# Order and grouping around the output products of a four-layer trunk on one core

## The chip, the core and the metric

The program runs on one core of one Trainium2 chip, in one launch. The metric is the device time of one execution in microseconds (us), from a host-side launch to completion. A profiled execution also leaves a trace: the span in it runs from the first to the last instruction of the program on the core.

Five engines work side by side, each with its own instruction stream, executed in order: PE (TensorE, matrix products and transposes), DVE (VectorE, elementwise work), ACT (ScalarE, functions of one operand and copies), POOL (GpSimd) and SP (SyncE, which here only issues DMA transfers).

## The reference, cut to what matters

A trunk of four layers on 256 tokens of width 1024, all in float32. Each layer has a token mixer and a gated feed-forward network (FFN), both fed with a normalised and modulated copy of the residual stream x:

```python
for i in range(DEPTH):                                   # 4 layers
    mod = c_act @ ada_w[i] + ada_b[i]                    # adaLN: 6 vectors of 1024
    sh1, sc1, g1, sh2, sc2, g2 = jnp.split(mod, 6, axis=-1)
    h = modulate(rmsnorm(x, mix_norm_g[i]), sh1, sc1)    # h*(1+scale)+shift
    y = mixer(h)                # layer 0, 3: gMLP; layer 1: latent attention; layer 2: HGRN2
    x = x + (1.0 + g1)[:, None, :] * y
    h = modulate(rmsnorm(x, ffn_norm_g[i]), sh2, sc2)
    x = x + (1.0 + g2)[:, None, :] * conv_ffn(h, ...)    # up 1024 -> 5632, conv, gate, down 2816 -> 1024
return rmsnorm(x, final_g)
```

Every mixer and every FFN ends in an output product into the residual stream: `go` for gMLP (2048 to 1024), `wo` for the other two mixers (1024 to 1024), `dn` for the FFN (2816 to 1024).

## The kernel before

**Split precision.** Each float32 factor is split into a high and a low part (`fp32r`), and a product is three matmuls (`mm3`): high by high, high by low, low by high. Activations are split by `split` (ACT makes the high part, DVE the low one). Weights come as units of 128 x 2048 float32 (1 MB, tile `raw`, five buffers) by SP's DMA queue, in the order of a list, `plan`. `conv_half` converts one half of a unit: ACT casts `wh` (L209), DVE subtracts for `wl` (L210); `wh` and `wl` have five buffers of 1024 columns each. `unit()` hands out the next unit and asks, ahead of use, for later loads and conversions.

**Order.** The code is written in one order, and a planner then decides the order on each engine with its own model of costs: of the instructions that it holds to be ready it takes the one written first, so an instruction written later can be placed ahead of earlier ones that it holds to be waiting. `tc.issue_after(ins)` forces every instruction of the block on the engine of `ins` to stand behind `ins` on that engine; it says nothing about other engines. `state["chain"]` holds such instructions for conversions.

**adaLN.** The modulation vectors are worked out beside the layers. Some (`ada_vector`) are computed on DVE, one instruction for 128 rows and 1024 columns (tile `adaw`, L339, two for each load of 1 MB), the others (`ada_tensor`) on PE as 16 narrow matmuls for each load (tile `adaps`, L317). `pacing`, called by `unit()`, loads and runs them at rates from a table; `need` runs all that a stage must have. `GAPS` gives, stage by stage, how many loads of the PE kind are kept back; `modulated` runs them at the join between two stages.

**A layer.** `modulated(l, which)` transposes the normalised x on PE (`xt`, L464), modulates (`nt`, L473, on DVE) and splits it into `hh` and `hlo`, in eight chunks of 128 features; while it does so, it asks for one half of a conversion. The mixer or the FFN follows. In `ffn` 22 chunks of `up` (48 matmuls of 256 columns each) go into four PSUM banks (`acc`), and ACT and DVE make the causal convolution, the gate and the split of each chunk (`y`, `g`, `gh`, `gl`, L1169 to L1175). The first step of a chunk that reads its bank starts when all of the chunk's matmuls are done.

**Output products.** The output is token-major: two token tiles of 128 and two halves of 512 columns, so four accumulators (`acc`, the same four banks). A unit of weights holds two K chunks of 128. `out_product` runs over the K chunks and, inside, over the four accumulators; only the last unit (in the last layer's `dn` the last two) goes accumulator by accumulator, and each finished one is passed to `residual`: multiply by the gate row (`gated`, L500), add to x (L501), squares (L502). After both halves of a token tile `root` works out the inverse root, and `scaled` writes the normalised tile to `gx`, half on DVE (L455), half on ACT (L456). `gx` holds, in its second half, the gate row: `gate_load` asks for it before the output product (in the `wo` products at their second unit), from ten buffers with the tag `big`.

Of the kernel before, what the change touches and what calls it, by code (L numbers as in the profile page):

```python
# [18 lines left out]
D = 1024  # L19
# [8 lines left out]
GAPS = [3, 0, 4, 3, 5, 3, 3, 0]  # L28
# [16 lines left out]
HGO = "o0 o1 s0 a0 o2 s1 a1 n0 o3 s2 n1 w0 s3 n2 w1 n3 w2 w3"  # L45
ADA_P = [(0, 5), (1, 2), (1, 3), (2, 4), (2, 5), (3, 2), (3, 5)]
# [44 lines left out]
def build(ctx, tc, A, out, stages=None):  # L91
# [99 lines left out]
    def conv_half():  # L191

        if not halves:
            if state["dma"] == state["conv"]:
                if state["dma"] == len(plan):
                    return
                dma_next()
            raw, n = raws.pop(0)
            ready.append([])
            halves.extend((raw, o, min(1024, n - o), state["conv"]) for o in range(0, n, 1024))  # L200
            state["conv"] += 1
        raw, o, w, n = halves.pop(0)
        wh = wp.tile([P, 1024], F32R, tag="wh", name=f"wh{n}_{o}", bufs=5)
        wl = wp.tile([P, 1024], F32R, tag="wl", name=f"wl{n}_{o}", bufs=5)
        with contextlib.ExitStack() as es:

            for ins in state["chain"]:
                es.enter_context(tc.issue_after(ins))
            act.copy(wh[:, :w], raw[:, o : o + w])  # L209
            i = dve.tensor_tensor(wl[:, :w], raw[:, o : o + w], wh[:, :w].bitcast(F32), op=ALU.subtract)  # L210
            state["sub"] = getattr(i, "ins", i)
        ready[-1].append((wh, wl))
# [114 lines left out]
    def ada_vector(l, u):  # L327
# [3 lines left out]
        def load(i):  # L331
# [3 lines left out]
            def run():  # L335
                for e in range(2):
                    b = 8 * u + 2 * i + e
                    c0 = col("ada_b", l * 48 + b)
                    dve.tensor_tensor_reduce(raw[:, e, :], raw[:, e, :], cbc[:], 1.0, prm[:, c0 : c0 + 1], ALU.mult, ALU.add,  # L339
                                             mod[:, l, b : b + 1])  # L340
                if i == 3:
                    mod_post(l, 8 * u, 8)
# [109 lines left out]
    def scaled(t, rs):  # L452

        xn = cur["gx"][:, t, :]
        dve.tensor_scalar_mul(xn[:, 0:512], x[:, t, 0:512], rs)  # L455
# [14 lines left out]
    def modulate_chunk(l, which, c, xt):  # L470
        b = 24 * which + c
        t = t1("nt")
        dve.tensor_scalar(t[:], xt, amul[:, l, which, c : c + 1], mod[:, l, b : b + 1], op0=ALU.mult, op1=ALU.add)  # L473
        split(hh[:, c, :], hlo[:, c, :], t[:])

    def modulated(l, which):
# [15 lines left out]
    def residual(t, f, ps, last):  # L492
# [7 lines left out]
        dve.tensor_tensor(g[:], ps, gx[:, 1, s], op=ALU.mult)  # L500
        dve.tensor_tensor(x[:, t, s], x[:, t, s], g[:], op=ALU.add)  # L501
# [30 lines left out]
    def out_product(name, k0, units, yh, yl, last, fin_=False):  # L532

        kcs = range(k0, k0 + 2 * len(units))
        if k0 == 0:
            cur["ps"] = [acc(f"{name}{i}") for i in range(4)]
        ps = cur["ps"]

        def one_(kc, t, f):
            a, b = hl(units[(kc - k0) // 2], kc % 2 * D + 512 * f, 512)  # L540
            ts = slice(t * P, t * P + P)
            mm3(ps[2 * t + f][:], yh(kc)[:, ts], yl(kc)[:, ts], a, b, kc == 0, kc == last)

        tf = [(t, f) for t in range(2) for f in range(2)]
        if last not in kcs:
            for kc in kcs:
                for t, f in tf:
                    one_(kc, t, f)
                if kc == k0:
                    flush(mid=1)  # L550
        else:

            for t, f in tf:
                for kc in kcs:
                    one_(kc, t, f)
                residual(t, f, ps[2 * t + f][:], fin_)

    def split(h, lo, src):
        act.copy(h, src)  # L559
        dve.tensor_tensor(lo, src, h.bitcast(F32), op=ALU.subtract)  # L560
# [84 lines left out]
    def gmlp(l, j, start=None):  # L645
# [91 lines left out]
        gate_load(l, 0)  # L737
        for i in range(8):
            w = unit(LAST if i == 7 else None)
            out_product("go", 2 * i, [w], yh, yl, 15)  # L740
# [189 lines left out]
    class OutProj:  # L930
# [5 lines left out]
        def step(self, i):  # L936
            if i == 1:
                gate_load(self.l, 0)
            w = unit(LAST if i == 3 else None)
            out_product("wo", 2 * i, [w], self.yh, self.yl, KC - 1)  # L940
# [219 lines left out]
    def ffn(l):  # L1160
        gh, gl = hilo("g", NF)
        for c in range(NF):
            ps = proj_pair(hk, lk, KC, f"up{c}", c < KOUT)
# [12 lines left out]
            split(gh(c), gl(c), g[:])  # L1176
# [9 lines left out]
        gate_load(l, 1)  # L1186
        i = 0
        while i < NF // 2:
            w = [unit(LAST if i == NF // 2 - 1 else None)]
            if last and i == NF // 2 - 2:  # L1190
                w.append(unit())
            out_product("dn", 2 * i, w, gh, gl, NF - 1, last)
            i += len(w)
# [35 lines left out]
    for kind, l in stages:  # L1229
# [3 lines left out]
        if kind == "mix":  # L1233
# [3 lines left out]
            if l % 3 == 0:  # L1237
                if quick:
# [4 lines left out]
                    def start(chunk):  # L1243
                        for step in FIRST.split():
# [10 lines left out]
                            if step[0] == "a":  # L1255
# [5 lines left out]
                                modulate_chunk(l, 0, c, xt[0][:, c % 2, :])  # L1261
# [112 lines left out]
```

## Time and profile before

| what | value |
|---|---|
| median of 3 runs | 1383.8 us (1382.55 to 1386.59) |
| the profiled execution's own time | 1384.63 us |
| its span, first to last instruction | 1382.8 us |
| mean granted TensorE clock | 0.985 |
| ACT busy | 776.2 us (56%) |
| POOL busy | 18.0 us (1%) |
| moved by DMA | 330.69 MB, mean 239 GB/s |

A line of the profile names the kernel line (L339), the engine, the operation and the tiles it writes and reads (`adaw<-adaw,cbc,prm`). A row of the timeline begins with the start and the duration in us from the start of the span; a number in brackets at its end is the idle time of the engine just before, and what ended it. The granted clock is the share of TensorE's full clock that the chip gave in that stretch; 0.50 is half speed. The end of a matmul is modelled, since matmuls overlap: start-to-start times tell how fast PE goes.

### The profile page before, as it was taken

How to read it: one execution, taken by the hardware profiler on the slowest of the kernel's cores; microseconds unless marked ns; L12 is line 12 of the kernel's file. 1: busy time of each engine (PE TensorE's matmuls, PEld its weight loads, DVE VectorE, ACT ScalarE, POOL GpSimd, SP SyncE). 2: the span in 40 equal slices, each digit the busy share in tenths (PEclk: the TensorE clock that was granted, in tenths of full speed). 3: DMA queues.
4: the chain of work that ended last, by engine and by line, in shares of the span. 5: the costliest groups of instructions: out<-in, count | busy, mean ns of one | idle time of the engine just before them, and what ended most of it. 6: DMA issues, size and time to landing. Idle time of an engine off the chain costs nothing.

```text
span 1382.8 us, 24847 instructions
## 1 busy us (share of the span) xinstructions
PE 1329.4 (96%) x10092; PEld 1195.7 (86%) x10092; DVE 1123.6 (81%) x1818; ACT 776.2 (56%) x1220; POOL 18.0 (1%) x27
## 2 busy tenths in 40 slices
PE   7999989999999999979999999999899999999997
PEld 6799779998787899968797879998777998899986
DVE  4699698888887889797878989889976874888854
ACT  3763366664456666534585646665445744666643
POOL 0100000000000000000000000000001000000000
PEclk8999999999999999999999999999999999999999
DMA  9868955566957366598565586567876465455640
GB/s 383 328 243 312 412 178 183 214 214 266 424 215 292 146 227 237 182 350 337 183 241 186 197 337 214 184 214 289 333 307 228 158 251 185 153 183 184 214 152 31
DMA packets 49162, 330.69 MB, mean 239 GB/s; under 512 B 6548, under 2 KB 7572, under 8 KB 10134
## 3 DMA queue, kind: packets, MB, share of 16 engines
q1 hardware_dynamic: 47888, 327.40, 63.0%
q10 hardware_dynamic: 1160, 1.71, 0.4%
q8 instruction: 79, 1.29, 0.4%
q14 instruction: 35, 0.29, 0.1%
HBM read 328.01 MB, written 1.08 MB: 238 GB/s over the span
## 4 chain that ended last, share of the span: by engine, by line
PE 56%; DVE 9%; ACT 2%; issue 1%; ACTq 0%; DVEq 0%
PE up L240 8%; PE up L241 8%; PE up L242 8%; PE dn L240 4%; PE dn L242 4%; PE dn L241 4%; DVE adaw L339 2%; DVE wl L210 1%; PE wo L240 1%; ACT wh L209 1%; PE wo L242 1%; PE wo L241 1%; PE v L240 1%; PE v L242 1%; PE v L241 1%
## 5 line engine op out<-in xcount | busy, mean ns | idle before, releaser
L209 ACT CAST wh<-raw 128x1024 fp32r<-128x1024 f32 x418 | 433.7, 1049 | 393.5 <-PE up L241 176.0
L210 DVE TENSOR_TENSOR wl<-raw,wh 128x1024 fp32r<-128x1024 f32 x418 | 508.9, 1227 | 147.7 <-ACT wh L209 146.8
L240 PE MATMUL up<-hh,wh 128*128 128x256 f32 x1408 | 398.4, 284 | 3.4 <-DVE y L1171 2.4
L241 PE MATMUL up<-hlo,wh 128*128 128x256 f32 x1408 | 398.0, 283 | 0.4 <-DVE hlo L560 0.2
L242 PE MATMUL up<-hh,wl 128*128 128x256 f32 x1408 | 398.0, 283 | 0.1
L240 PEld LDWEIGHTS up<-hh,wh 128*128 128x128 f32 x1408 | 269.9, 192 | 5.6 <-issue 3.9
L241 PEld LDWEIGHTS up<-hlo,wh 128*128 128x128 f32 x1408 | 270.1, 192 | 1.0 <-DVE hlo L560 0.9
L242 PEld LDWEIGHTS up<-hh,wl 128*128 128x128 f32 x1408 | 270.3, 192 | 0.5 <-DVE wl L210 0.3
L339 DVE CUSTOM_DVE_ANT_0 adaw<-adaw,cbc,prm 128x1024 f32<-128x1024 f32 x120 | 151.7, 1277 | 2.7 <-DMA adaw<-adad 2.7
L240 PE MATMUL dn<-wh,gh 128*128 128x512 f32 x352 | 139.5, 398 | 13.3 <-DVE y L1171 11.8
L241 PE MATMUL dn<-wl,gh 128*128 128x512 f32 x352 | 139.1, 395 | 0.6 <-DVE wl L210 0.6
L242 PE MATMUL dn<-wh,gl 128*128 128x512 f32 x352 | 139.2, 395 | 0.0
L1169 ACT ACTIVATE y<-up,cwb 128x256 f32<-128x256 f32 x176 | 98.6, 560 | 20.8 <-DVE y L1171 20.5
L240 PEld LDWEIGHTS dn<-wh,gh 128*128 128x128 f32 x352 | 67.5, 192 | 29.9 <-issue 12.5
L1171 DVE SCALAR_TENSOR_TENSOR y<-up,cwb,y 128x254 f32<-128x254 f32 x176 | 84.7, 481 | 5.0
L1170 DVE SCALAR_TENSOR_TENSOR y<-up,cwb,y 128x255 f32<-128x255 f32 x176 | 84.0, 477 | 2.5 <-ACT y L1169 2.5
L241 PEld LDWEIGHTS dn<-wl,gh 128*128 128x128 f32 x352 | 67.4, 191 | 14.9 <-DVE wl L210 1.1
L242 PEld LDWEIGHTS dn<-wh,gl 128*128 128x128 f32 x352 | 67.2, 191 | 14.3
L240 PE MATMUL u<-hh,wh 128*128 128x256 f32 x256 | 74.0, 289 | 0.0
L241 PE MATMUL u<-hlo,wh 128*128 128x256 f32 x256 | 72.4, 283 | 0.0
L242 PE MATMUL u<-hh,wl 128*128 128x256 f32 x256 | 72.4, 283 | 0.0
L240 PE MATMUL v<-wh,hh 128*128 128x512 f32 x128 | 51.9, 408 | 3.0 <-ACT hh L559 2.5
(331 smaller groups left out, 2052.3 us busy)
## 6 DMA issues: line engine op xcount, KB each, us to landing
raw<-up SPq DMA_DIRECT2D x88, 1024.0 KB
adaw<-adad SPq DMA_DIRECT2D x60, 1024.0 KB
raw<-dn SPq DMA_DIRECT2D x44, 1024.0 KB
adaw<-adap SPq DMA_DIRECT2D x28, 1024.0 KB
raw<-gmu SPq DMA_DIRECT2D x16, 1024.0 KB
raw<-gmo SPq DMA_DIRECT2D x16, 1024.0 KB
raw<-gmv SPq DMA_DIRECT2D x15, 1024.0 KB
adaf<-ada SPq DMA_DIRECT2D x8, 1024.0 KB
```

The lines of the kernel that those rows point to most:

```text
L209: act.copy(wh[:, :w], raw[:, o : o + w])
L210: i = dve.tensor_tensor(wl[:, :w], raw[:, o : o + w], wh[:, :w].bitcast(F32), op=ALU.subtract)
L240: pe.matmul(ps, lh, rh, start=start, stop=False)
L241: pe.matmul(ps, lh, rl, start=False, stop=False)
L242: i = pe.matmul(ps, ll, rh, start=False, stop=stop)
L339: dve.tensor_tensor_reduce(raw[:, e, :], raw[:, e, :], cbc[:], 1.0, prm[:, c0 : c0 + 1], ALU.mult, ALU.add, mod[:, l, b : b + 1])
L1169: act.activation(y[:], ps[:, e, :], AF.Identity, bias=b, scale=w[2])
L1170: dve.scalar_tensor_tensor(y[:, 1:], ps[:, e, : S - 1], w[1], y[:, 1:], op0=ALU.mult, op1=ALU.add)
L1171: dve.scalar_tensor_tensor(y[:, 2:], ps[:, e, : S - 2], w[0], y[:, 2:], op0=ALU.mult, op1=ALU.add)
```

## The change

- **First unit tile by tile.** In all output products the first unit runs accumulator by accumulator over its two K chunks; before, only the last did.
- **Chunks held at the end.** In `go` and `dn` the last three K chunks (four in the last layer's `dn`, as before) run accumulator by accumulator with `residual` behind each; before, two. The `wo` products still hold two.
- **Gate asked for later.** `gate_load` comes four units before the end of `go` and `dn` instead of before their first unit, and at the third unit of `wo` instead of the second. For the FFN `gx` now lies in a `raw` buffer.
- **`scaled`.** Token tile 0 is scaled by DVE alone, in one instruction of 1024 columns.
- **Order constraints.** In `residual` the first multiplication stands behind the last conversion and the last adaLN update written so far on DVE, each later one behind the addition before it. Conversions written after the first two chunks of `modulated` stand behind those chunks' modulation (DVE) and high part (ACT). In `ffn` the conversions and DVE's adaLN updates written in chunk c stand behind the last DVE step (`gl`) of chunk c-2. At the start of the program the conversions' DVE step stands behind the modulation of chunk 0.
- **`GAPS`** of layer 0's `dn` goes from 0 to 2.

```diff
-GAPS = [3, 0, 4, 3, 5, 3, 3, 0]
+GAPS = [3, 2, 4, 3, 5, 3, 3, 0]
+HOLD = (3, 4)
 ...
 # conv_half, after act.copy(wh)
+            if "sub1" in state:
+                es.enter_context(tc.issue_after(state["sub1"]))
 ...
 # gate_load
-        gx = cur["gx"] = big("gx", (P, 2, D))
+        if which:
+            gx = wp.tile([P, 2, D], F32, tag="raw", name="gx", bufs=NRAW)
+        else:
+            gx = big("gx", (P, 2, D))
+        cur["gx"] = gx
 ...
 # ada_vector
+                    with contextlib.ExitStack() as es:
+                        for ins in state["chain"]:
+                            es.enter_context(tc.issue_after(ins))
+                        r = dve.tensor_tensor_reduce(raw[:, e, :], ...)
+                    state["ada"] = getattr(r, "ins", r)
 ...
 # scaled
+        if t == 0:
+            dve.tensor_scalar_mul(xn, x[:, t, :], rs)
+            return
 ...
 # modulated
-                modulate_chunk(l, which, c, xts[i][:, c - c0, :])
+                ins = modulate_chunk(l, which, c, xts[i][:, c - c0, :])
+                if c < 2:
+                    state["chain"] += ins
 ...
 # residual
-        dve.tensor_tensor(g[:], ps, gx[:, 1, s], op=ALU.mult)
-        dve.tensor_tensor(x[:, t, s], x[:, t, s], g[:], op=ALU.add)
+        with contextlib.ExitStack() as es:
+            for k in ("sub", "ada") if t == f == 0 else ("add",):
+                if k in state:
+                    es.enter_context(tc.issue_after(state[k]))
+            dve.tensor_tensor(g[:], ps, gx[:, 1, s], op=ALU.mult)
+        i = dve.tensor_tensor(x[:, t, s], x[:, t, s], g[:], op=ALU.add)
+        state["add"] = getattr(i, "ins", i)
 ...
-    def out_product(name, k0, units, yh, yl, last, fin_=False):
+    def out_unit(n, w, ps, yh, yl, i):
+        kcs = range(2 * i, 2 * i + 2)
+        order = [(kc, t, f) for t, f in TF for kc in kcs] if i == 0 else [(kc, t, f) for kc in kcs for t, f in TF]
+        for j, (kc, t, f) in enumerate(order):
+            chunk_product(n, w[kc % 2], ps, yh, yl, kc, t, f)
+            if j == 3:
+                flush(mid=1)
+    def out_end(n, held, ps, yh, yl, last=False):
+        for t, f in TF:
+            for j, w in enumerate(held):
+                chunk_product(n, w, ps, yh, yl, n - len(held) + j, t, f)
+            residual(t, f, ps[2 * t + f][:], last)
+    def tokens(units, name, yh, yl, l, which, last=False):
+        ps = [acc(f"{name}{i}") for i in range(4)]
+        held = []
+        for i in range(units):
+            if i == units - 4:
+                gate_load(l, which)
+            w = unit(LAST if i == units - 1 else None)
+            if i < units - 2:
+                out_unit(2 * units, w, ps, yh, yl, i)
+            else:
+                held += w
+                while len(held) > HOLD[last] - 2 * (units - 1 - i):
+                    for t, f in TF:
+                        chunk_product(2 * units, held[0], ps, yh, yl, 2 * units - 2 * (units - 1 - i) - len(held), t, f)
+                    held.pop(0)
+        out_end(2 * units, held, ps, yh, yl, last)
 ...
 # gmlp: the loop over out_product becomes
+        tokens(8, "go", yh, yl, l, 0)
 # OutProj.step
-            if i == 1:
+            if i == 2:
                 gate_load(self.l, 0)
 ...
 # ffn
+        done = []
         for c in range(NF):
+            if c > 1:
+                state["chain"] = (done[c - 2],)
 ...
-            split(gh(c), gl(c), g[:])
+            done.append(split(gh(c), gl(c), g[:])[1])
 ...
-        gate_load(l, 1)
-        i = 0
-        while i < NF // 2:
-            ...
+        tokens(NF // 2, "dn", gh, gl, l, 1, last)
```

More of the change, by code (lines that the diff above doesn't have):

```diff
@@ L530, in finish, with chunk_product @@
             (nc.scalar if f else nc.sync).dma_start(out[:, t, s], y[:, t, s])
-    def out_product(name, k0, units, yh, yl, last, fin_=False):
[L534 to L556, printed above, removed]
+    def chunk_product(n, w, ps, yh, yl, kc, t, f):
+        s = slice(512 * f, 512 * f + 512)
+        ts = slice(t * P, t * P + P)
+        mm3(ps[2 * t + f][:], yh(kc)[:, ts], yl(kc)[:, ts], w[0][:, s], w[1][:, s], kc == 0, kc == n - 1)
@@ new lines, in build @@
+    TF = [(t, f) for t in range(2) for f in range(2)]
+    def out_unit(n, w, ps, yh, yl, i):
[10 more added lines that the diff above has]
+            residual(t, f, ps[2 * t + f][:], last)
@@ L736, in gmlp @@
         pace("go", l)
[L737 to L740, printed above, removed]
+        tokens(8, "go", yh, yl, l, 0)
     tables = []
@@ L936, in step @@
         def step(self, i):
-            if i == 1:
+            if i == 0:
+                self.ps = [acc(f"wo{j}") for j in range(4)]
+            if i == 2:
                 gate_load(self.l, 0)
             w = unit(LAST if i == 3 else None)
-            out_product("wo", 2 * i, [w], self.yh, self.yl, KC - 1)
+            if i < 3:
+                out_unit(KC, w, self.ps, self.yh, self.yl, i)
+            else:
+                out_end(KC, w, self.ps, self.yh, self.yl)
     def hg_units():
```

21 lines of the change are left out of this document (9 added, 12 removed).

## The prediction

> **What bounds the kernel now.** I read the page first, for which engine fills the span.
>
> ```profile
> span 1382.8 us, 24847 instructions
> PE 1329.4 (96%) x10092; PEld 1195.7 (86%) x10092; DVE 1123.6 (81%) x1818; ACT 776.2 (56%) x1220; POOL 18.0 (1%) x27
> ...
> L210 DVE TENSOR_TENSOR wl<-raw,wh 128x1024 fp32r<-128x1024 f32 x418 | 508.9, 1227 | 147.7 <-ACT wh L209 146.8
> L339 DVE CUSTOM_DVE_ANT_0 adaw<-adaw,cbc,prm 128x1024 f32<-128x1024 f32 x120 | 151.7, 1277 | 2.7 <-DMA adaw<-adad 2.7
> ```
>
> TensorE (PE) is busy for 96%, DVE for 81%, and the diff removes none of its work. What can be won is time in which PE waits, and time in which it runs slowly. So the second view is the list of waits (columns: microseconds in total, times, longest).
>
> ```profile
> PE dn L240 <- DVE y L1171: 11.8, 5, 4.5
> PE xt L464 <- DVE gx L455: 8.6, 6, 5.4
> ...
> PE up L240 <- DVE y L1171: 2.4, 6, 0.4
> ...
> ACT wh L209 <- DMA raw<-gmo: 24.3, 8, 5.3
> ```
>
> The largest wait stands where a feed-forward layer changes from `up` to `dn`, the second at the joins, where an output product ends and the next stage needs its normalised input. The third view is the table by stretches, asked where I found the granted clock (after the busy times of PE, weight load, DVE, ACT and POOL) at one half; the last row is an undisturbed stretch.
>
> ```profile
> 178.40:185.10 6.70, 4.51 (x19) 3.63 (x19) 5.67 (x15) 6.29 (x14) 0.00 (x0) 0.50 0.16 65
> 608.50:615.10 6.60, 4.28 (x10) 3.44 (x11) 6.60 (x14) 0.74 (x2) 0.00 (x0) 0.50 0.96 395
> 680.20:683.40 3.20, 3.16 (x13) 2.92 (x14) 3.18 (x9) 1.60 (x4) 0.39 (x2) 0.50 0.44 184
> 970.30:973.50 3.20, 3.20 (x9) 2.53 (x8) 3.20 (x8) 0.41 (x1) 0.00 (x0) 0.50 1.00 420
> 977.20:980.40 3.20, 3.20 (x9) 2.55 (x8) 2.49 (x7) 1.27 (x3) 0.00 (x0) 0.50 0.93 361
> ...
> 630.00:668.00 38.00, 38.00 (x169) 31.48 (x168) 27.36 (x32) 14.24 (x14) 0.00 (x0) 1.00 0.83 314
> ```
>
> Each half-speed stretch stands at a wait, so a wait is paid twice: once idle, once slow.
>
> **Part 1, `up` to `dn`: the leash in `ffn`, the late gate, the first unit tile by tile.** The timeline of DVE and PE at layer 1, and two PE rows of layer 2:
>
> ```profile
> 608.60 0.48 DVE L1170 SCALAR_TENSOR_TENSOR y<-up,cwb,y 128x255 f32<-128x255 f32 x1
> 608.99 1.28 DVE L339 CUSTOM_DVE_ANT_0 adaw<-adaw,cbc,prm 128x1024 f32<-128x1024 f32 x1
> ...
> 602.63 0.47 PE L240 MATMUL dn<-wh,gh 128*128 128x512 f32 x1 [1.43 <-ACT y L1169]
> 610.82 0.77 PE L240 MATMUL dn<-wh,gh 128*128 128x512 f32 x1 [4.53 <-DVE y L1171]
> 618.00 0.47 PE L240 MATMUL dn<-wh,gh 128*128 128x512 f32 x1 [1.45 <-DVE y L1171]
> ...
> 969.00 0.47 PE L240 MATMUL dn<-wh,gh 128*128 128x512 f32 x1 [2.95 <-DVE y L1171]
> 976.78 0.54 PE L240 MATMUL dn<-wh,gh 128*128 128x512 f32 x1 [2.52 <-DVE y L1171]
> ```
>
> The four `dn` accumulators are the PSUM banks of the last four `up` chunks, and a bank is free only when DVE has read it for y. Between two steps of one y stands an adaLN update (adaw, L339), which nothing needs yet. DVE is three chunks behind when PE begins `dn`. Layer 1 loses 1.43 + 4.53 + 1.45 = 7.4 us idle and, at half clock, half of the 4.28 us worked, 2.1: 9.5. Layer 2 loses 2.95 + 2.52 = 5.5 and half of 3.20 + 3.20, 3.2: 8.7. Together 18.2.
>
> After the change, conversions and updates asked for in chunk c stand behind the last DVE step of chunk c-2, so DVE can be at most two chunks late. The leash lasts through `dn` at chunk 19, so updates can still fall between the y steps of chunks 20 and 21. The first `dn` unit needs its last bank after three tiles instead of after three matmul triples: at six matmuls of 0.225 us each (rows further down) 4.05 us instead of 2.0. The y of chunk 21 takes two ACT and four DVE steps, about 2.6 us by the 0.48 of the row; with three updates of 1.28 in its gaps 6.4. That is 2.35 us late, in two layers 4.7. Gain 18.2 - 4.7 = **13.5**; ends 0 (as many updates as before) and 18.2. The updates moved are not removed: they go to the rest of `dn`, where the undisturbed row has 38 - 27.36 = 10.6 us of free DVE for about eight of them. If that cover fails they stand before the join (part 4).
>
> Near the end of layer 1's `up`, PE waits 0.41 us in every chunk for the y of three chunks before. The leash removes that lag: gain **2.4** (ends 0 and 2.4).
>
> **Part 2, joins: three chunks held, order of residual, conversions behind the first chunks.** The join after `dn` of layer 1:
>
> ```profile
> 672.55 0.39 PE L242 MATMUL dn<-wh,gl 128*128 128x512 f32 x1
> ...
> 674.92 1.29 DVE L339 CUSTOM_DVE_ANT_0 adaw<-adaw,cbc,prm 128x1024 f32<-128x1024 f32 x1
> 675.06 0.71 ACT L456 ACTIVATE gx<-x,ss 128x512 f32<-128x512 f32 x1
> 676.20 1.27 DVE L339 CUSTOM_DVE_ANT_0 adaw<-adaw,cbc,prm 128x1024 f32<-128x1024 f32 x1
> 676.95 2.92 ACT L209 CAST wh<-raw 128x1024 fp32r<-128x1024 f32 x3
> ...
> 679.78 0.81 ACT L559 CAST hh<-nt 128x256 fp32r<-128x256 f32 x2
> 680.24 0.58 PE L240 MATMUL hf<-hh,wh 128*128 128x256 f32 x1 [1.32 <-ACT hh L559]
> ```
>
> From PE's end at 672.94 to the first product of the next stage 7.3 us pass. In the chain stand two updates, the ACT half of token tile 0 (0.71, ahead of tile 1's root) and three casts of later weights ahead of hh. The change puts the last traced update and conversion ahead of the first residual, the whole of token tile 0 on DVE (about 0.9 us by the row's two halves, beside PE's longer tiles: nine matmuls, 2.03 us, against 1.4 of DVE), and later conversions behind hh of chunk 1. The cleanest join is after `go` in layer 3:
>
> ```profile
> 1181.32 0.39 PE L242 MATMUL go<-wh,yl 128*128 128x512 f32 x1
> 1181.64 1.93 PE L317 MATMUL adaps<-adaw,cact 128*32 128x256 f32 x32
> ...
> 1186.97 0.51 PE L240 MATMUL up<-hh,wh 128*128 128x256 f32 x2
> ```
>
> It takes 5.26 us with tile 0's half still on ACT; without that about 0.4 less: 4.9 is the chain itself, and what I take for the joins that are long now. The other two long ones:
>
> ```profile
> 172.94 2.35 DVE L210 TENSOR_TENSOR wl<-raw,wh 128x1024 fp32r<-128x1024 f32 x2
> 174.18 0.39 PE L240 MATMUL go<-wh,yh 128*128 128x512 f32 x1
> 174.63 0.39 PE L242 MATMUL go<-wh,yl 128*128 128x512 f32 x1
> 180.37 1.46 PE L464 MATMUL xt<-ident,gx 128*128 128x128 f32 x5 [5.36 <-DVE gx L455]
> 184.47 0.80 PE L240 MATMUL up<-hh,wh 128*128 128x256 f32 x2
> ...
> 375.39 0.55 PE L464 MATMUL xt<-ident,gx 128*128 128x128 f32 x3 [2.11 <-DVE gx L455]
> 380.78 0.38 PE L240 MATMUL cq<-hh,wh 128*128 128x256 f32 x1
> ```
>
> (Two matmuls lie between 174.18 and 174.63, hence 0.225 us each.) After `go` in layer 0, 175.01 to 184.47 is 9.46 us; in it two conversions sit between the first product and its addition, which the new order forbids. To 4.9 it is 4.6 less; idle of that size still costs clock, 1.1 of it: **3.5**. After `dn` of layer 0, 373.28 to 380.78, 7.5 to 4.9: **2.6**. After `dn` of layer 1, 2.4 and the half-clock stretch at 680.20 (1.6): **4.0**. The two `wo` joins hold two chunks as before and the one after `dn` of layer 2 has its gap filled; I take 0.5 each for the ACT half that leaves: **1.5**. After `go` in layer 3, 0.4 is won, but the 32 filler matmuls shown there are used up earlier (GAPS for layer 0's `dn` goes from 0 to 2, where they fill the 2.11 us wait), and an unfilled gap falls to half clock for 3.2 us: 0.4 - 1.6 = **-1.2**. Sum of the joins **10.4**; ends 3 (only ACT's half is won, in seven places) and 16 (no clock loss, updates all in time).
>
> On what a gap does to the clock: the 2.11 us wait above is followed by half speed, as the stretches show for longer ones. [...]
>
> **Part 3, the start.** The first weight conversion is put behind nt of chunk 0.
>
> ```profile
> 14.27 0.80 PE L240 MATMUL v<-wh,hh 128*128 128x512 f32 x1 [2.24 <-ACT hh L559]
> ```
>
> The wait of 2.24 holds one conversion of 1.23 on DVE; about 1 us earlier, at half clock still: **0.5** (ends -0.5, since wl then comes later for the second matmul, and 1).
>
> **Part 4, what it costs.** In `dn`, gx takes one of the five raw buffers from four units before the end until the transposes are done; on SP's queue a weight load that finds no buffer holds back every load behind it, updates' weights and gate rows included. The nearest row for late weights is that of gmo, at most 5.3 us for one cast, where PE does not stop. I take 0.5 in each of four layers, **2.0** (ends 0 and 5.3 each). The first residual now waits on DVE for the last update and the last conversion; behind it queue the other residuals and the root. If two updates (2.55) come late in the joins after `dn` of layers 0 to 2, the longer tiles take back most of it; I take 0.8 each, **2.4** (ends 0 and 7.6). The gate asked for later has over 20 us until its use in `dn` and `go` (four units of 24 matmuls, 21.6 us); in `wo` only about two units, covered as long as SP isn't held: 0.
>
> Sum: 13.5 + 2.4 + 10.4 + 0.5 - 2.0 - 2.4 = **22.4** less. The profiled execution took 1384.6 us (span 1382.8 and 1.8 around it), 0.8 above the median of the three runs. Forecast 1384.6 - 22.4 = 1362.2, some 1361.5 on the scale of the median.
>
> **The rivals.**
> *The updates stay in the way.* The planner fills every gap between two dependent DVE steps; nothing ties updates to chunks 20 and 21. If two thirds of the losses of part 1 remain (gain 6 instead of 13.5) and the residuals wait their full price (7.6 instead of 2.4), the time is 1361.5 + 7.5 + 5.2 = 1374. For it: the alternation in the rows; against it: the lag of three chunks, which gave the updates their place, is cut.
> *The leash turns round (slower).* Conversions now wait for DVE's own backlog. If in `up` PE comes to wait for wl instead of y, each of 4 x 20 leashed chunks pays; from 22.4 / 80 = 0.28 us a chunk on, the change loses. At the 0.41 that the wait of the other sort cost, 33 us: 1361.5 + 33 = 1394. Against it: the chunks are 6 us, and the step waited for ends some 4 us into the chunk before the one that traces the conversion.
> *Weights come late.* With four buffers in place of five, a cast 5.3 us late at the end of each `dn` eats 19 of the 22: 1381, no change that could be told.
> *Everything fits.* All upper ends: 18.2 + 2.4 + 16 + 1 = 37.6: 1346.
>
> **How the numbers follow.** Forecast 0.64, updates stay 0.16, everything fits 0.08, weights late 0.06, leash 0.06. The range 1345 to 1377 holds the first three (0.88) less some tails. Under 0.3%, 4 us, nothing can be told from no change here. Faster 0.64 + 0.16 + 0.08 = 0.88, same 0.06, slower 0.06.
>
> **What would show it.** Right: no wait of PE dn for y above 1 us; DVE at the end of `up` with y steps back to back, and updates behind gl of chunk 19; no PE wait for y inside `up`; 4.9 us from the last output matmul to the first of the next stage; L455 with a 1024-wide form, half as many L456; fewer stretches at 0.50. Wrong: PE up waiting for wl; L500 waiting for adaw or wl in the first tile; casts waiting for DMA near the ends of `dn`.

## The result and the profile after

The changed kernel takes 1353.02 us (median of 4 runs, 1352.72 to 1353.39); the kernel before, on the same chip, 1383.84 (1382.55 to 1386.59). The ratio is 0.9775, 95% interval 0.9758 to 0.9792: some 31 us, or 2.2%, less. I had forecast 1361.5 and a range of 1345 to 1377. The time lies in the range and the sign is right; the gain is 30.8 where the sum gave 22.4.

The page of the changed kernel, and the top of its list of waits on PE (microseconds in total, times, longest), with two short rows from further down the list:

```profile
span 1351.2 us, 24627 instructions
PE 1316.6 (97%) x10092; PEld 1192.5 (88%) x10092; DVE 1112.7 (82%) x1818; ACT 773.5 (57%) x1212; POOL 17.3 (1%) x27
```

```profile
PE xt L478 <- DVE gx L467: 8.0, 4, 3.9
PE xt L478 <- DVE gx L469: 3.1, 3, 2.4
...
PE up L245 <- DVE wl L213: 0.9, 2, 0.5
...
PE dn L243 <- DVE y L1217: 0.5, 2, 0.3
```

The lines have moved: matmuls L240 to L242 are now L243 to L245, wl L210 is L213, the updates L339 are L349, y is L1216 and L1217, gx L467, L469 and L470. The 11.8 us that `dn` waited for y are 0.5, and the row of `up` waiting for y (2.4) is gone. The waits at the joins are as long as before: 8.0 and 3.1 against 8.6 and 1.1. So nearly all of the change lies between `up` and `dn`. I measured each product from the start of its first matmul to the end of its last in both traces, and each join between them (us):

| piece | before | after |
|---|---|---|
| `up`, layer 1 / 2 | 131.2 / 127.3 | 128.0 / 127.0 |
| idle between `up` and `dn`, layer 1 | 1.4 | none |
| `dn`, layer 1 / 2 | 70.3 / 70.2 | 60.5 / 60.6 |
| `go` / `dn`, layer 0 | 49.3 / 60.2 | 47.9 / 62.1 |
| joins after `go` and `dn` of layer 0 | 9.5, 7.5 | 7.5, 7.3 |
| joins after `wo` and `dn` of layer 1 | 6.2, 7.3 | 4.7, 4.7 |
| joins after `wo` and `dn` of layer 2 | 6.2, 6.2 | 7.1, 4.7 |
| join after `go` of layer 3 | 5.3 | 5.6 |
| first product starts at | 14.3 | 13.4 |

Layers 1 and 2 from `up` to `dn` give 24.5 us, the joins 6.5, the start 0.9. The other pieces take 0.4 more in all, and the span is 31.5 shorter.

**`up` to `dn`.** The timeline of DVE at layer 1, and PE's one wait there:

```profile
593.73 1.28 DVE L349 CUSTOM_DVE_ANT_0 adaw<-adaw,cbc,prm 128x1024 f32<-128x1024 f32 x1
...
596.53 0.48 DVE L1217 SCALAR_TENSOR_TENSOR y<-up,cwb,y 128x254 f32<-128x254 f32 x1
...
599.52 0.42 DVE L600 TENSOR_TENSOR gl<-g,gh 128x256 fp32r<-128x256 f32 x1
599.86 0.48 DVE L1216 SCALAR_TENSOR_TENSOR y<-up,cwb,y 128x255 f32<-128x255 f32 x1
...
601.77 1.28 DVE L349 CUSTOM_DVE_ANT_0 adaw<-adaw,cbc,prm 128x1024 f32<-128x1024 f32 x1
...
604.57 0.48 DVE L1217 SCALAR_TENSOR_TENSOR y<-up,cwb,y 128x254 f32<-128x254 f32 x1
...
605.20 0.47 PE L243 MATMUL dn<-wh,gh 128*128 128x512 f32 x1 [0.18 <-DVE y L1217]
```

The updates do still stand between the steps of the last two chunks, as the first rival said, with conversions beside them. The last y ends at 605.05, 10.4 us after the end of `up` at 594.6. But PE stands only 0.18 us: it ran 45 matmuls of `dn` first, which I read as 15 on each of three banks that were free by then. In the kernel before it ran 15, waited 4.53 us, ran 15 more and waited 1.45 us.

**The clock**, as stretches (PE, weight load, DVE, ACT, POOL, granted clock, DMA share, GB/s):

```profile
177.50:180.90 3.40, 3.32 (x16) 3.32 (x17) 2.73 (x8) 2.25 (x6) 0.00 (x0) 0.51 0.00 0
375.50:378.80 3.30, 2.97 (x16) 2.79 (x14) 2.63 (x7) 2.15 (x4) 0.00 (x0) 0.50 1.02 429
1153.80:1157.00 3.20, 3.20 (x15) 3.20 (x16) 2.61 (x7) 2.10 (x5) 0.00 (x0) 0.50 0.02 5
594.60:605.10 10.50, 10.42 (x47) 8.29 (x45) 10.50 (x20) 2.90 (x6) 0.00 (x0) 1.00 0.91 328
```

The half-speed stretches of layers 1 and 2 are gone. Besides those at the program's start and end three stay, at the three joins that still have a gap of over 2 us (3.85, 3.70 and 2.36).

**Two joins side by side.** After `go` of layer 0, then after `dn` of layer 1:

```profile
170.11 0.69 DVE L522 TENSOR_TENSOR gated<-go,gx 128x512 f32<-128x512 f32 x1 [3.92 <-PE go L245]
...
174.32 0.68 DVE L522 TENSOR_TENSOR gated<-go,gx 128x512 f32<-128x512 f32 x1
...
176.64 0.55 PE L478 MATMUL xt<-ident,gx 128*128 128x128 f32 x3 [3.85 <-DVE gx L467]
177.58 3.04 PE L478 MATMUL xt<-ident,gx 128*128 128x128 f32 x13 [0.39 <-DVE gx L469]
180.27 0.56 PE L243 MATMUL up<-hh,wh 128*128 128x256 f32 x1
...
649.23 0.68 DVE L522 TENSOR_TENSOR gated<-dn,gx 128x512 f32<-128x512 f32 x1
...
655.05 2.80 PE L324 MATMUL adaps<-adaw,cact 128*32 128x256 f32 x48
655.16 0.69 DVE L522 TENSOR_TENSOR gated<-dn,gx 128x512 f32<-128x512 f32 x1 [0.62 <-PE dn L245]
...
657.78 2.07 PE L478 MATMUL xt<-ident,gx 128*128 128x128 f32 x16
659.84 0.38 PE L243 MATMUL hf<-hh,wh 128*128 128x256 f32 x1
```

In layer 1 only the fourth `gated` is left when PE is done (655.16), fillers cover the gap, and 4.71 us pass. In layer 0 PE ends at 176.64 - 3.85 = 172.79 and the fourth `gated` starts 1.5 us later. The first one, which waits for PE, starts only 2.7 us before PE's end, against 5.9 us in layer 1. I read this as the planner running the four accumulators' last matmuls mixed, so that they end close together (the trace doesn't tell the accumulators apart; experiment 5 puts the tiles in order). The fillers it has put into the product instead of the gap. The next fence shows where they went after `dn` of layer 0, 13 us ahead of its join:

```profile
358.34 1.93 PE L324 MATMUL adaps<-adaw,cact 128*32 128x256 f32 x32
```

### The profile page after: what moved, and what is told of

It is laid out like the page before. It is cut to its first block, busy times and chain, and to the rows that moved or that the text cites. A ratio compares the mean times of both kernels' runs of the same rounds, so it can differ in the third digit from the quotient of the medians.

```text
span 1351.2 us, 24627 instructions
## 1 busy us (share of the span) xinstructions
PE 1316.6 (97%) x10092; PEld 1192.5 (88%) x10092; DVE 1112.7 (82%) x1818; ACT 773.5 (57%) x1212; POOL 17.3 (1%) x27
## 4 chain that ended last, share of the span: by engine, by line
PE 85%; DVE 9%; ACT 3%; issue 1%; DMA 1%; ACTq 0%; DVEq 0%
PE up L245 12%; PE up L243 12%; PE up L244 12%; PE dn L243 5%; PE dn L245 5%; PE dn L244 5%; PE u L244 2%; PE u L243 2%; PE u L245 2%; DVE wl L213 2%; PE v L243 2%; PE v L244 2%; PE v L245 2%; PE go L243 2%; PE go L244 2%; PE go L245 2%
## 5 line engine op out<-in xcount | busy, mean ns | idle before, releaser
L210 ACT CAST wh<-raw 128x1024 fp32r<-128x1024 f32 x418 | 432.8, 1048 | 324.0 <-PE up L244 110.9
L213 DVE TENSOR_TENSOR wl<-raw,wh 128x1024 fp32r<-128x1024 f32 x418 | 507.2, 1225 | 84.6 <-ACT wh L210 83.8
L245 PE MATMUL up<-hh,wl 128*128 128x256 f32 x1408 | 397.8, 283 | 0.9 <-DVE wl L213 0.9
L243 PE MATMUL up<-hh,wh 128*128 128x256 f32 x1408 | 397.7, 284 | 0.0
L245 PEld LDWEIGHTS up<-hh,wl 128*128 128x128 f32 x1408 | 270.4, 192 | 1.3 <-DVE wl L213 1.3
L243 PEld LDWEIGHTS up<-hh,wh 128*128 128x128 f32 x1408 | 270.0, 192 | 0.6 <-issue 0.4
L349 DVE CUSTOM_DVE_ANT_0 adaw<-adaw,cbc,prm 128x1024 f32<-128x1024 f32 x120 | 151.3, 1282 | 0.3 <-DMA adaw<-adad 0.3
L245 PE MATMUL dn<-wh,gl 128*128 128x512 f32 x352 | 136.8, 389 | 0.0
L243 PE MATMUL dn<-wh,gh 128*128 128x512 f32 x352 | 134.7, 390 | 0.5 <-DVE y L1217 0.5
L1216 DVE SCALAR_TENSOR_TENSOR y<-up,cwb,y 128x255 f32<-128x255 f32 x176 | 84.5, 480 | 34.0 <-ACT y L1215 33.5
L1217 DVE SCALAR_TENSOR_TENSOR y<-up,cwb,y 128x254 f32<-128x254 f32 x176 | 84.1, 478 | 1.5
L243 PEld LDWEIGHTS dn<-wh,gh 128*128 128x128 f32 x352 | 66.0, 188 | 15.2 <-issue 1.7
L245 PEld LDWEIGHTS dn<-wh,gl 128*128 128x128 f32 x352 | 66.1, 188 | 13.7
L244 PEld LDWEIGHTS dn<-wl,gh 128*128 128x128 f32 x352 | 66.1, 188 | 13.5
L243 PE MATMUL u<-hh,wh 128*128 128x256 f32 x256 | 74.0, 289 | 0.0
L245 PE MATMUL u<-hh,wl 128*128 128x256 f32 x256 | 72.4, 283 | 0.0
L600 DVE TENSOR_TENSOR gl<-g,gh 128x256 fp32r<-128x256 f32 x88 | 37.1, 421 | 22.1 <-ACT gh L599 20.5
```

The source lines that it names most:

```text
L243: pe.matmul(ps, lh, rh, start=start, stop=False)
L244: pe.matmul(ps, lh, rl, start=False, stop=False)
L245: i = pe.matmul(ps, ll, rh, start=False, stop=stop)
L349: r = dve.tensor_tensor_reduce(raw[:, e, :], raw[:, e, :], cbc[:], 1.0, prm[:, c0 : c0 + 1], ALU.mult, ALU.add, mod[:, l, b : b + 1])
L600: b = dve.tensor_tensor(lo, src, h.bitcast(F32), op=ALU.subtract)
L1216: dve.scalar_tensor_tensor(y[:, 1:], ps[:, e, : S - 1], w[1], y[:, 1:], op0=ALU.mult, op1=ALU.add)
```

## The experiments

My theory after the result: the leash in `ffn` is the main thing, by what it does to updates and conversions together; the order in `residual` is second; the held chunks and the first unit tile by tile do little, since the planner rearranges PE anyway; the joins of layer 0 are long because fillers and tiles are misplaced, which can be mended. Each kernel ran with the kernel before on its chip (medians 1383.8 to 1384.4).

**1. The leash alone, and all but the leash.**

```diff
 # leash_only: the kernel before with these lines in ffn (done filled as in the change),
 # and ada_vector's updates tied to state["chain"] as in the change
+            if c > 1:
+                state["chain"] = (done[c - 2],)
 # no_leash: the changed kernel without these two lines
-            if c > 1:
-                state["chain"] = (done[c - 2],)
```

> The kernel before with one part of the change: in ffn, conversions and DVE's adaLN updates of chunk c stand behind gl of chunk c-2. Theory (order on DVE at the up to dn step was the main loss): the stretch from the start of up to the end of dn in layers 1 and 2 shortens by 20 to 25 us in all, time 1359 to 1364. Rival (the late gate, or the first unit tile by tile, gives PE the room): the leash alone leaves the waits of dn for y at 5 us or more, time 1375 or above.

> The changed kernel without the leash in ffn, all else kept. Theory: the waits of dn for y in layers 1 and 2 come back, time 1370 to 1378. Rival (late gate or tile by tile is enough): 1353 to 1358.

Measured: leash_only 1364.02 us (ratio 0.9851, 0.9833 to 0.9869), no_leash 1381.45 (0.9983, 0.9973 to 0.9994). PE's waits in the first, then in the second:

```profile
PE dn L240 <- DVE y L1178: 0.5, 2, 0.3
```

```profile
PE dn L243 <- DVE y L1215: 11.1, 5, 4.5
PE xt L478 <- DVE gx L467: 8.0, 4, 3.9
...
PE up L243 <- DVE y L1215: 2.4, 6, 0.4
```

The leash alone takes away the waits of `dn` and gives 20 of the 31 us; `dn` of layer 1 is 60.5 without any other part. From the start of `up` to the end of `dn`, layers 1 and 2 take 24.8 us less, all that the whole change gives there. The other parts together give 2.6; that run took 3 us more than I had expected at most. The two gains add up to 22.7, 8 short of the whole. In the profiled executions the shortfall is 7.1, and it's spread: 2.5 in the joins after `dn` of layers 1 and 2, 3.1 in `dn` of layers 0 to 2, 2.5 in layer 2's mixer, the rest in smaller pieces of both signs. For the two joins the traces show a reason: with the leash alone they grow to 8.0 us each (7.3 and 6.2 before), while the whole change has 4.7. Work that the leash moves out of `up` can reach a join there. DVE of leash_only after `dn` of layer 2:

```profile
1007.82 1.22 DVE L210 TENSOR_TENSOR wl<-raw,wh 128x1024 fp32r<-128x1024 f32 x1
...
1009.62 1.28 DVE L503 TENSOR_TENSOR gated<-dn,gx 128x512 f32<-128x512 f32 x2
```

PE is done with `dn` at 1008.2; a conversion runs across its end, and two of the four products follow it. In the whole change the order in `residual` forbids that (experiment 3). I haven't run the leash with that order alone.

**2. The leash on conversions alone.** The same kernel as after, but updates aren't tied:

```diff
-                        for ins in state["chain"]:
-                            es.enter_context(tc.issue_after(ins))
                         r = dve.tensor_tensor_reduce(...)
```

> The changed kernel in which DVE's adaLN updates are no longer tied to state['chain']; conversions still stand behind gl of chunk c-2. Theory A (the updates between the y steps are what made PE wait): dn of layers 1 and 2 goes back to 65 us or more each, time 1362 to 1374. Theory B (the lag of three chunks, made by conversions run ahead, is the cause, and the updates only fill gaps): dn stays at 60 to 62 us, time 1352 to 1357.

Measured: 1369.31 us (0.9894, 0.988 to 0.9909), so 16 of the 31 us are lost, which is theory A's time. In the trace 11.6 us of the loss lie between `up` and `dn` of layers 1 and 2, and 2.2 in the join after `dn` of layer 1, since the edit frees the updates at the joins too. `dn` itself takes 64.0 and 64.2, a little under the 65 that I had set for it.

```profile
PE dn L244 <- DVE wl L213: 4.1, 2, 2.1
PE up L245 <- DVE wl L213: 3.8, 5, 1.3
...
PE dn L243 <- DVE y L1215: 2.6, 2, 1.3
```

Both must be tied. With the conversions alone on the leash, updates take the gaps ahead of them, and PE waits more for wl (7.9 us) than for y (2.6): the mechanism of my slower rival, at a price of 7.9 us and not 33, and only where the leash is cut in half.

**3. The order in `residual`, and the conversions behind the first chunks.**

```diff
 # no_order, in residual
-            for k in ("sub", "ada") if t == f == 0 else ("add",):
-                if k in state:
-                    es.enter_context(tc.issue_after(state[k]))
 # no_modchain, in modulated
-                if c < 2:
-                    state["chain"] += ins
```

> The changed kernel without the order constraints in residual (last conversion and last update ahead of the first product, each product behind the addition before it). Theory: they keep updates and conversions out of the joins; the joins after dn of layers 1 and 2 go from 4.7 us to 6 or more, that after go of layer 0 by 2, time 1357 to 1361. Rival (the conversions behind the first chunks and the missing ACT half do it alone): 1352 to 1355.

> The changed kernel in which conversions asked for in modulated and later are not tied to the first two chunks. Theory: casts of weights slip ahead of hh on ACT again, 0.5 to 1.5 us in each of seven joins, time 1357 to 1363. Rival (no cast is ready that early, since wh buffers are held): 1352 to 1354.

Measured: no_order 1362.08 us (0.9841, 0.9825 to 0.9857), 9 more than the change and 1 more than I had expected at most; no_modchain 1354.63 (0.9792, 0.9776 to 0.9808), between the two expectations and not separated from the change by its interval. DVE and PE of no_order after `go` of layer 0:

```profile
171.29 0.69 DVE L519 TENSOR_TENSOR gated<-go,gx 128x512 f32<-128x512 f32 x1 [7.61 <-PE go L245]
171.90 2.35 DVE L213 TENSOR_TENSOR wl<-raw,wh 128x1024 fp32r<-128x1024 f32 x2
174.17 0.68 DVE L520 TENSOR_TENSOR x<-x,gated 128x512 f32<-128x512 f32 x1
...
179.60 3.97 PE L478 MATMUL xt<-ident,gx 128*128 128x128 f32 x16 [5.63 <-DVE gx L467]
```

The two conversions are back between the first product and its addition, as before the change, and the join takes 9.25 us. Those after `dn` of layers 0 and 2 take 9.2 and 7.1; the one after `dn` of layer 1 takes 5.3, less than the 6 that I had expected. The constraint keeps conversions out of the joins, as part 2 of the prediction said. The conversions behind the first chunks matter in one join, after `dn` of layer 1 (6.7 against 4.7), about what no_modchain lost.

**4. The parts that rearrange PE, and the gate.**

```diff
 # hold2
-HOLD = (3, 4)
+HOLD = (2, 4)
 # no_tile, in out_unit
-        order = [(kc, t, f) for t, f in TF for kc in kcs] if i == 0 else [...]
+        order = [(kc, t, f) for kc in kcs for t, f in TF]
 # gate_old: gate_load at unit 0 (in wo at unit 1), and
-            gx = wp.tile([P, 2, D], F32, tag="raw", name="gx", bufs=NRAW)
+            gx = big("gx", (P, 2, D))
 # scaled_split, in scaled
-        if t == 0:
-            dve.tensor_scalar_mul(xn, x[:, t, :], rs)
-            return
```

> The changed kernel with two K chunks held at the end of go and dn, as before, instead of three. Theory (at a join the chain behind the last tile sets the time, and DVE keeps up with tiles of two chunks): within 1 us of the changed kernel in each of five joins, time 1353 to 1356. Rival (the longer tiles are what shortens the joins): 1.4 us or more in each of five joins, 1359 to 1362.

> The changed kernel with the first unit of every output product K chunk by K chunk, as before, all else kept. Theory (the planner moves PE's matmuls among the banks that are free, whichever way they are written): layers 1 and 2 keep dn at about 60.5 us each and the time is 1352 to 1354. Rival (the order of the first unit is what lets PE pass the late y steps, as the prediction's 4.05 against 2.0 us had it): two layers wait about 2 us more each and it takes 1357 or more.

> The changed kernel with the gate row asked for where it was before (ahead of the first unit of go and dn, at the second unit of wo) and gx in a big buffer. Theory (the late gate and the raw buffer neither cost nor bring time, since PE waited for no weights in dn): within 1.5 us of the changed kernel, 1352 to 1354. Rival 1 (the gate row's early transfer held back the start of dn): the first dn matmuls of layers 1 and 2 wait again and it takes 1356 or more. Rival 2 (the raw buffer that gx takes costs the 2 us that the prediction allowed for it): 1350 to 1351.5.

> The changed kernel with token tile 0 scaled half on DVE and half on ACT, as before, all else kept. Theory of the prediction (the ACT half of tile 0 lies on the chain of a join with 0.4 to 0.7 us): up to seven joins get about 0.5 us longer, 1354 to 1357. Rival (tile 0's scaling lies beside PE's last output matmuls, only tile 1's is on the chain): no change, 1352.5 to 1353.5.

Measured: hold2 1352.51 us (0.9774, 0.9759 to 0.9788), no_tile 1353.3 (0.9779, 0.9762 to 0.9796): neither differs from the change. In both `dn` of layers 1 and 2 stays at 60.5 and 60.6; in hold2 the joins after `go` and `dn` stay within 0.1 us, and in no_tile PE's waits in `dn` and at the joins are the same to a tenth. The third held chunk and the first unit tile by tile are worth nothing that can be seen here.

gate_old 1355.53 (0.9796, 0.978 to 0.9811). All three expectations missed: 2.5 us more than the change, its interval just overlapping, and `dn` of layers 1 and 2 untouched. The difference lies elsewhere. `go` of layer 0 takes 49.3 instead of 47.9, with the same 48 fillers in it cut into smaller groups; the joins after `wo` of layer 1 and `dn` of layer 2 take 0.9 and 0.6 more and `up` of layer 3 1.3 more; smaller pieces give 1.9 back. The late gate isn't what freed `dn`, and the raw buffer costs nothing that can be seen; whether these 2.5 us are more than the planner's chance placement stays open.

scaled_split 1356.59 (0.9805, 0.9788 to 0.9822), 3.6 more, inside what the prediction's theory gave; its interval just touches the change's. Its join after `dn` of layer 1:

```profile
658.61 0.71 ACT L467 ACTIVATE gx<-x,ss 128x512 f32<-128x512 f32 x1
...
659.54 0.16 DVE L459 RECIPROCAL ss<-ss 128x1 f32<-128x1 f32 x1 [0.99 <-ACT ss L458]
```

and the same place of the changed kernel:

```profile
657.69 0.16 DVE L459 RECIPROCAL ss<-ss 128x1 f32<-128x1 f32 x1 [0.25 <-ACT ss L458]
```

Tile 1's root waits for ACT's half of tile 0, 0.99 against 0.25. Three joins grow by 0.47 to 0.48, the one after `dn` of layer 0 by 0.3, the other three by 0.04 or less or shrink. In all 1.5 us are in the joins, of the 2.9 by which the two profiled executions differ; the rest lies between them, most of it in layer 1's mixer, and I can't assign it.

**5. Mending the joins.** Fillers kept behind the last output matmul (fill), in addition a GAPS entry cut (fill_gaps), in addition each of the last tiles behind the one before (grouped):

```diff
 # fill, in modulated
-        while loaded["p"]:
-            ada_run("p")
+        with tc.issue_after(state["mm"]):          # the last matmul written
+            while loaded["p"]:
+                ada_run("p")
 # fill_gaps
-GAPS = [3, 2, 4, 3, 5, 3, 3, 0]
+GAPS = [3, 2, 4, 3, 3, 3, 3, 0]
 # grouped, in out_end, from the second tile on
+                if k:
+                    es.enter_context(tc.issue_after(state["mm"]))
```

> The changed kernel, in which the narrow adaLN matmuls kept back for a join stand on PE behind the last output matmul (the planner had put those of the joins after go and dn of layer 0 into the output products). Theory (there the join is an empty gap of 3.7 us that also costs half clock): the products of layer 0 shorten by 2 to 3 us each, the joins keep their length or lose 1 to 2 us of half clock; time 1345 to 1349. Rival (the fillers only push the transposes back, and the clock falls all the same): 1352 to 1354.

> The kernel 'fill' (fillers behind the last output matmul) with GAPS for layer 2's mixer at 3 instead of 5, so that the join after its output product has 48 narrow matmuls instead of 80 and the join after go of layer 3 has some again. Theory (the first join is limited by PE's own work, the second by idle and half clock): 7.1 to 5.2 us and 5.3 to 4.9 us, time 1342 to 1344.5 against 1346.7 of 'fill'. Rival (the matmuls only change places): 1346 to 1347.5.

> This is the kernel with both filler edits (fillers behind the last output matmul on PE, five kept-back loads turned into three for layer 1's second join), 1345.14 us, and one more constraint: in out_end each of the last three tiles' matmuls stands behind the previous tile's last matmul on PE, so that the planner can't bunch the four tiles' ends. Theory (in the joins after go and dn of layer 0 the first products came late because the planner mixed the tiles): the join after go of layer 0 goes from 6.20 to about 4.8, the one after dn of layer 0 from 6.04 to about 4.7, the four gated products start some 5.9, 4.0, 2.0 us before and right at PE's end as they do after dn of layer 1, and the time is 1342 to 1344. Rival (the planner mixed the tiles because the low part wl of the last chunk is late): the joins get shorter but PE waits for wl inside the last tiles for as long or longer, 1345 to 1348.

Measured: fill 1346.69 us (0.9726, 0.9709 to 0.9742), fill_gaps 1345.14 (0.9719, 0.9704 to 0.9733), grouped 1342.84 (0.9706, 0.9691 to 0.9721). The join after `go` of layer 0 in fill_gaps, with the clock of its stretch:

```profile
168.32 2.80 PE L324 MATMUL adaps<-adaw,cact 128*32 128x256 f32 x48
172.24 0.77 PE L478 MATMUL xt<-ident,gx 128*128 128x128 f32 x5 [1.12 <-DVE gx L467]
173.18 1.42 PE L478 MATMUL xt<-ident,gx 128*128 128x128 f32 x11 [0.17 <-DVE gx L469]
174.59 0.39 PE L243 MATMUL up<-hh,wh 128*128 128x256 f32 x1
```

```profile
171.00:177.00 6.00, 4.63 (x35) 3.68 (x31) 5.27 (x13) 4.56 (x9) 0.00 (x0) 1.00 0.77 325
```

The same 48 fillers that made `go` 47.9 us long now stand in the gap; `go` takes 43.8, the join 6.2, and the clock stays at 1.00. Together that is 5.4 us in this one place (fill has the same). Fillers beyond the gap only lengthen it: in the join after `wo` of layer 2 the change issues 26 + 32 + 22, fill_gaps 26 + 22, and the join goes from 7.1 to 5.4. The medians of fill and fill_gaps differ by 1.6, less than I had expected and not separated by their intervals. The join after `dn` of layer 0, which the second edit doesn't touch, takes 7.3 in fill and 6.0 in fill_gaps, since the clock fell in one and not in the other (last section).

In grouped, the product's end and its join after `go` of layer 0:

```profile
160.67 0.50 PE L244 MATMUL go<-wl,yh 128*128 128x512 f32 x1 [0.20 <-DVE wl L213]
...
161.80 0.50 PE L244 MATMUL go<-wl,yh 128*128 128x512 f32 x1 [0.16 <-DVE wl L213]
...
171.34 2.08 PE L478 MATMUL xt<-ident,gx 128*128 128x128 f32 x16
173.40 0.38 PE L243 MATMUL up<-hh,wh 128*128 128x256 f32 x1
```

Theory and rival are both half right. The two joins of layer 0 take 4.7 and 5.0 instead of 6.2 and 6.0, but `go` and `dn` ahead of them take 1.0 us more each, both with two waits for wl near their ends. In fill_gaps, with the tiles as the planner has them, the same stretches have no wait. Net in the two places: 0.6 us. The intervals of grouped and fill_gaps overlap; both are below the changed kernel's whole interval, so some 8 to 10 us more are there to be had.

## Why the prediction was right, and where its sum was off

The sign, the range and the place are right; the term sizes are off in both directions, and the sum came out 8 us short. That it came no further off is partly luck: what the joins lacked offset part of what the other terms gave beyond the sum.

- **Up to dn: 13.5 + 2.4 forecast, 24.5 measured**, above even my upper ends of 20.6. Two steps failed. The remaining stall, 4.7, was 0.5, but not by my reasoning. In layer 1 the last y came 10.4 us after the end of `up` and not 6.4, since conversions stand in its gaps too. And I had PE run through the first unit in the order written, 4.05 us with six matmuls for each tile, but it ran 45 matmuls, 10.2 us, on the three free banks (no_tile shows that the order written is of no account). The two errors cancelled, which is luck. And the 18.2 us of loss were too few. `dn` of layers 1 and 2 shrank by 9.8 and 9.6 and 1.4 of idle went, 20.8 in all, since I had summed only the waits for y and half of the slow stretches that showed; the traces hold more in the same stretch, such as

```profile
965.32 0.50 PE L241 MATMUL dn<-wl,gh 128*128 128x512 f32 x1 [0.65 <-DVE wl L210]
```

  of the kernel before, a wait for a conversion late for the same reason, and in layer 1's `dn` ten fillers that now stand in the join. The wait inside layer 1's `up` was worth 2.4 by its rows; that `up` got 3.2 shorter.
- **Joins: 10.4 forecast** (8.0 with the 2.4 that part 4 took back)**, 6.5 measured.** Three joins, after `wo` of layer 1 and `dn` of layers 1 and 2, came down to 4.7, about the 4.9 that I took for the chain itself; for two of them I had forecast only 0.5 each, and they gave 1.5. After `dn` of layer 1 the join gave 2.6; the half-clock stretch, 1.6 of my 4.0, lay in the mixer behind it, which got 1.0 shorter. The join after `wo` of layer 2 got 0.8 longer, with more fillers in it. The step that failed was to give the same 4.9 to the joins of layer 0, which save 2.0 and 0.2 where I had 3.5 and 2.6. The new order does keep conversions out (no_order), but the tiles end mixed and the fillers aren't in the gap. I had written that GAPS for layer 0's `dn` fills its 2.11 us wait; the 32 fillers ran inside the product, which got 1.9 longer, and the gap stayed. After `go` of layer 3 the gap opened as I had said, but the join got 0.4 longer and I had 1.2; by the clock that falls in it, the same order takes 4.8 to 5.6 us there in other runs (no_leash, no_order, no_tile).
- **`scaled`: about 0.5 a join**, 0.47 measured in three (scaled_split). The instruction itself, my 0.9 from two halves, takes 0.75:

```profile
L467 DVE TENSOR_SCALAR gx<-x,ss 128x1024 f32<-128x1024 f32 x8 | 6.0, 752 | 0.0
```

- **Start: 0.5 forecast, 0.9 measured.**
- **What it costs: 4.4 forecast, nothing seen.** One cast in layer 0's `dn` does wait 9.0 us for its weights, which the list shows as new, but PE doesn't stop for it:

```profile
ACT wh L210 <- DMA raw<-dn: 24.9, 6, 9.0
```

  In six of the eight output products the first `gated` step waits for neither an update nor a conversion: DVE stands idle ahead of it, for PE, 3.92 us after `go` of layer 0 (the fence of the two joins). After `dn` of layer 1 and `go` of layer 3 it follows a conversion without idle time, so a wait is possible there, but the first of these joins is one of the three at 4.7.
- **The rivals.** *Updates stay in the way* was right in what it saw and wrong in its price, since PE had other banks. *The leash turns round* needs the updates free: with them 7.9 us of waits for wl, in the change 0.9. *Weights late* didn't happen to PE. *Everything fits*, 1346, is what the fillers in the gaps reach (1345.14), by another way.
- **The clock.** I left in the loss after gaps of some 2 us. In the kernel before, the gap of 2.11 us after `dn` of layer 0 is followed by half speed (0.50 from 376.40 to 379.60). In the changed kernel the gap after `go` of layer 3 shows it: five transposes, 2.36 us idle, then half speed (0.50 from 1153.80 to 1157.00, above).

```profile
1150.66 0.77 PE L478 MATMUL xt<-ident,gx 128*128 128x128 f32 x5 [0.24 <-DVE gx L467]
1153.79 2.61 PE L478 MATMUL xt<-ident,gx 128*128 128x128 f32 x11 [2.36 <-DVE gx L469]
```

  But such a gap needn't do it. In no_leash the same place has the same transposes and the same idle time, and the clock stays at 1.00 throughout; the eleven transposes take 1.42 us there, 2.61 above:

```profile
1181.73 1.42 PE L478 MATMUL xt<-ident,gx 128*128 128x128 f32 x11 [2.36 <-DVE gx L469]
1183.14 0.38 PE L243 MATMUL up<-hh,wh 128*128 128x256 f32 x1
```

  The transposes alone don't tell such cases apart: the wait of 2.52 us in layer 2 of the kernel before (976.78 in the prediction) has no transpose in it and half speed follows at 977.0, and in the stretch at 375.50 above all but one of PE's 16 instructions are transposes, and full clock follows. The stretches at half clock are 3.4 us long here and 6.8 in layer 1 before, one and two steps of the grid that the traces show; it is in the last section, with the work of PE that a step held where the clock fell.

## What to carry to other kernels

Before trimming an engine's work, look at what stands between two dependent steps of the chain that frees a buffer: tying all such later work, conversions and updates alike, to a step two chunks back gave 20 of 31 us, and leaving the updates free lost 16 of the whole 31. A late step cost only what the waiting engine couldn't fill with other work (the last y came 10.4 us after the end of `up`, and PE, with 45 matmuls on the banks that were free, stood 0.18 us), so count the other free buffers before pricing a wait. A filler must be held to its gap, or a planner can spend it earlier: here that lengthened the product (47.9 us against 43.8) and left the gap to idle (3.85 us) and, in some executions, half clock (0.51 after that idle time).

## What the hardware showed that I had not expected

- With narrow fillers (32 output columns, 48 in 2.80 us) followed by 1.12 us of idle and 16 transposes the granted clock stayed at 1.00 (fill_gaps, 171 to 177 us), where in the changed kernel 3.85 us of idle in the same place was followed by a stretch at 0.51 (177.50 to 180.90).
- The same fillers cost more here when they were scattered: against 43.8 us with all 48 in the gap (fill_gaps), `go` of layer 0 took 4.1 us longer with them in three groups (47.9, the changed kernel) and 5.5 in the seven groups of gate_old (49.3).
- In these traces the granted clock changes on a grid. The record of the clock in the trace of the kernel before has it fall or rise at 608.40, 615.23, 970.22, 973.63, 977.04 and 980.46; all the distances are multiples of 3.413 us (970.22 - 608.40 is 106 of them). In the changed kernel it falls or rises at 177.45, 180.87, 375.43, 378.84, 1153.66 and 1157.08, by the same steps (1153.66 - 177.45 is 286 of them), with the grid 2.5 us later in the span. So where a gap falls on the grid counts. In these two traces PE was busy for 1.64 us or less in 13 of the recorded steps at full clock, and half speed followed each; all the others held 1.85 us or more, and full clock followed. The wait of 1.45 us that ended at 618.00 fell in a step with 1.96 us of work (615.23 to 618.64), the one of 2.52 that ended at 976.78 in a step with 0.89 (973.63 to 977.04). After `dn` of layer 0, fill and fill_gaps issue the same 32 fillers and 16 transposes with some 2.2 us of idle between them. In fill one step of the grid (366.22 to 369.64) holds 1.23 us of PE's work, and half speed follows; in fill_gaps the steps hold 1.66 and 2.86 us, and the clock stays at 1.00. A single join from one execution can be off by such a stretch, here 1.3 us.
